# Chunk sums first in the linear attention, spills through other queues, and another opening, in a hybrid attention block

## The chip, the core and the metric

The kernel runs on one core of a Trainium2 chip. The metric is the device time of one execution in microseconds (us); lower is better. TensorE (PE) multiplies matrices, VectorE (DVE), ScalarE (ACT) and GpSimd (POOL) work element by element, and transfers are issued from the queues of SyncE (SP), ACT or POOL. Each engine runs its own instructions strictly in the order in which they stand in its program, and an instruction that has to wait holds back all that stand behind it.

## What is computed

One decoder block on 1024 tokens of width 1024: a softmax attention with low-rank queries and keys (8 heads), beside a gated linear attention (4 heads, keys of 128, values of 256), whose outputs are gated, merged, projected and added to x.

```python
h = rmsnorm(x, g_in)
(c_q, c_kv, k_r, z_mla, q_g, k_g, v_g, a_lr, z_gla, gate_mla, gate_gla) = split(h @ w_in)
# softmax attention: q, k, v from c_q, c_kv (both normalised) and the rotated k_r, causal
y_mla = (softmax_attention(q, k, v) * silu(z_mla)) @ w_proj_mla
# linear attention, head by head, chunk by chunk, b = cumsum of log decay in the chunk
q_in = q_g * exp(b); k_in = k_g * exp(-b); k_st = k_g * exp(b_last - b)
attn = (q_in @ k_in.T) * causal
o = attn @ v_g + q_in @ state                    # within the chunk, and from all before it
state = exp(b_last) * state + k_st.T @ v_g       # from chunk to chunk
y_gla = (rmsnorm(o, g_gla) * silu(z_gla)) @ w_proj_gla
merged = sigmoid(gate_mla) * y_mla + sigmoid(gate_gla) * y_gla
out = rmsnorm(x + merged @ w_out, g_final)
```

Inputs and outputs are float32.

## The kernel before

Every product is taken in three matmuls on a value's rounded part and its remainder (hi·hi, hi·lo, lo·hi); `split` makes the two, the rounded part on ACT (L193) and the remainder on DVE (L194), and for weights `split_raw` (L170, L171, the remainder on DVE or POOL). The 1024 tokens are two halves of 512 (index h). The kernel goes through five stages.

**The opening** (`blocks`, L390 to L505). x is loaded in 16 tiles of 128x512. While they come, PE multiplies zeros 26 times (NWARM, L395). For each half, `squares` squares the eight tiles on ACT and adds them on DVE, `scales` sums over the partitions on PE (L424) and raises the mean to the power -1/2 on POOL (L241), and `spread` copies the row over the partitions on PE (L246). `norm` (L440) scales a tile on DVE and `split` cuts it. The second half's squares stand right behind the first half's tiles in the program.

**The products** (L384). h @ w_in for everything but the gates, by a seven-product scheme on 2x2 blocks whose rows are the token halves; the first two kinds of products (i = 1 and 2) of eight pairs of weight tiles are made early, while the second half of x is still being normalised (`x_steps`), and are spilled to HBM as m1d and c11d. `product` makes twelve matmuls; the results go through `out_q`, `out_k`, `out_v`, `out_silu`, `out_misc` and `out_lat`, which scale, split and transpose them and spill them to HBM (gqd, gvd, szd, crd, latd, krd), through POOL's queue.

**The linear attention** (`core`, L1043 to L1127). Eight groups (two halves of four heads, four chunks of 128 tokens each). `fetch` brings a group's q, k, transposed k and v from HBM by five transfers of 512 KB on POOL's queue, two groups deep. `core` is a generator: scores of the four chunks (tile at), mask and split; then for each chunk its sum k_st.T @ v (tile ups), the outputs of the chunk before (tile ops), and the state (sm, st, split into sh and sl, three slots each); then the norm of the outputs (L241 on POOL, L1113 on ACT); then transposes, the gate, a split (uhl) and a spill of both parts to ugd on POOL's queue. Two groups are advanced in turns, one piece of each per round, and in three rounds of four one step of other work is put in.

That other work is a `Stream` of units, one per weight tile, that yields after every six matmuls. `gate_unit` multiplies x by a tile of the output gates (24 matmuls of 128x512 in four steps); GATES says how many of the 16 gate units of each half stand in front of the units uqr, uv and hi0 to hi3 (which make rotated queries, values, and the queries and keys of a pair of heads), and behind each hi. Fences hold a unit back until its inputs are there.

**The softmax attention** of each half runs over 8 heads: `row_max` of the next head, `scores`, exponentials, `values`, with stream steps between them; before the first head, `row_max(0)` is advanced with one step after each piece. From head 5 on, `linear_inputs` reads ugd back, already split, through POOL's queue. **The end** of each half multiplies by w_proj_gla, w_proj_mla and w_out (units yg, ym, wo).

The kernel's text says what each engine does and in roughly which order; a scheduler then places each engine's instructions by its own timeline of the program. `issue_after` puts instructions behind a given one on their engine.

## Time and profile before

| | |
|---|---|
| time, median of 3 runs | 1120.99 us (1116.2 to 1122.19) |
| the profiled execution | 1117.03 us |
| its span in the trace | 1115.3 us |
| PE, DVE, ACT, POOL busy | 1038.7, 774.5, 583.1, 354.1 us |
| TensorE's clock granted, mean | 0.961 of full speed |

The span goes from the first to the last instruction, and 1.7 us of the profiled execution lie around it. Busy time of PE counts each matmul to its modelled end, so that matmuls overlap; how much work there is shows better in how far apart matmuls start when nothing holds them up. The five stages follow each other on PE: the opening to 36.4 us, the products to 392.7, the linear attention until the first score of the softmax attention at 553.5, the softmax attention and the end of half 0 until about 803, and those of half 1.

### The profile page before, as it was taken

What the parts mean: (1) busy time and instruction counts of PE and PEld (TensorE: products, weight loads), DVE (VectorE), ACT (ScalarE), POOL (GpSimd) and SP (SyncE); (2) the same over time, 40 slices, a digit from 0 to 9 for tenths busy, and PEclk for the clock granted to TensorE, in tenths of its full rate; (3) what the DMA queues carried; (4) which work ended last, traced back from release to release, by engine and by line L of the source; (5) the groups of instructions that cost most, each with busy time, mean ns of one, the idle gap of its engine ahead of it and who ended that gap; (6) DMA issues with size and microseconds to landing.
All of it is one profiled execution on the core that took longest, in us unless ns stands there. A gap on an engine that the chain in (4) does not pass through costs nothing.

```text
span 1115.3 us, 14164 instructions
## 1 busy us (share of the span) xinstructions
PE 1038.7 (93%) x4794; PEld 845.5 (76%) x4794; DVE 774.5 (69%) x1309; ACT 583.1 (52%) x1074; POOL 354.1 (32%) x398
## 2 busy tenths in 40 slices
PE   7999998999999998977699999999899999999995
PEld 4888887878888877766477777888688787777774
DVE  6886667797877666776866766476856768767562
ACT  6644455566565335557666653245556566543332
POOL 0311211111111132532444522323555556432420
PEclk7899999999999999969899999999999999999998
DMA  6652646655645499998733637754933335425331
GB/s 238 217 191 90 228 156 226 232 190 194 216 164 196 170 361 336 339 310 288 256 119 93 212 123 274 255 160 145 201 112 97 105 97 172 153 72 190 122 114 76
DMA packets 80249, 208.74 MB, mean 187 GB/s; under 512 B 8704, under 2 KB 21376, under 8 KB 80048
## 3 DMA queue, kind: packets, MB, share of 16 engines
q1 hardware_dynamic: 47840, 105.18, 29.4%
q0 software_dynamic: 27728, 94.26, 25.2%
q10 hardware_dynamic: 4608, 8.39, 2.0%
q8 instruction: 38, 0.62, 0.2%
q14 instruction: 35, 0.29, 0.1%
HBM read 139.77 MB, written 68.03 MB: 186 GB/s over the span
## 4 chain that ended last, share of the span: by engine, by line
PE 69%; DVE 11%; ACT 7%; issue 6%; DMA 4%; POOL 2%; SPq 0%; POOLq 0%; ACTq 0%; DVEq 0%
PE prod L384 26%; PE pj L184 24%; PE y L895 2%; PE y L894 2%; PE y L893 2%; DMA wraw<-in_dram 2%; DVE pl L1270 2%; PE sc L1257 1%; DVE mx L1220 1%; PE sc L1259 1%; PE sc L1260 1%; PE ov L1279 1%; PE ov L1278 1%; PE sc L1213 1%; DMA xr<-in_dram 1%
## 5 line engine op out<-in xcount | busy, mean ns | idle before, releaser
L184 PE MATMUL pj<-xl,whi 128*128 128x512 f32 x384 | 137.1, 405 | 2.5 <-ACT xl L193 2.1
L170 ACT CAST whi<-wraw 128x1024 fp32r<-128x1024 f32 (+2 forms) x84 | 84.9, 1013 | 84.8 <-PE pj L184 59.9
L1272 POOL TENSOR_TENSOR acc<-acc,p 128x512 f32<-128x512 f32 (+3 forms) x80 | 83.2, 1040 | 111.5 <-ACT p L1266 97.6
L184 PE MATMUL pj<-xh,whi 128*128 128x512 f32 x256 | 104.7, 409 | 3.5 <-ACT whi L170 2.4
L171 POOL TENSOR_TENSOR wlo<-wraw,whi 128x1024 fp32r<-128x1024 f32 (+2 forms) x35 | 78.6, 2247 | 65.3 <-ACT whi L170 35.1
L1270 DVE TENSOR_TENSOR pl<-p,ph 128x512 fp32r<-128x512 f32 (+3 forms) x80 | 73.2, 921 | 31.5 <-ACT ph L1269 31.1
L184 PEld LDWEIGHTS pj<-xl,whi 128*128 128x128 f32 x384 | 75.2, 196 | 18.3 <-ACT xl L193 2.5
L703 DVE TENSOR_TENSOR ring<-prod,ring 128x512 f32<-128x512 f32 x85 | 58.2, 686 | 37.8 <-PE prod L384 37.6
L171 DVE TENSOR_TENSOR wlo<-wraw,whi 128x1024 fp32r<-128x1024 f32 x49 | 63.4, 1297 | 16.4 <-ACT whi L170 16.2
L1266 ACT ACTIVATE p<-sc 128x512 f32<-128x512 f32 (+3 forms) x80 | 37.3, 469 | 68.9 <-DVE sc L1262 46.9
L184 PE MATMUL pj<-lat,whi 128*128 128x512 f32 x264 | 70.2, 400 | 0.7 <-DVE vm L810 0.7
L184 PE MATMUL pj<-xh,wlo 128*128 128x512 f32 x256 | 69.6, 393 | 0.0
L193 ACT CAST w7h<-sw 128x512 fp32r<-128x512 f32 x68 | 42.1, 620 | 50.0 <-PE prod L384 42.1
L1220 DVE TENSOR_REDUCE mx<-sc 128x1 f32<-128x512 f32 (+2 forms) x96 | 52.3, 552 | 21.4 <-PE sc L1213 20.1
L184 PEld LDWEIGHTS pj<-xh,whi 128*128 128x128 f32 x256 | 50.0, 195 | 14.2 <-ACT whi L170 2.8
L384 PE MATMUL prod<-xh,w7h 128*128 128x512 f32 x136 | 56.6, 416 | 2.5 <-ACT ring L715 1.5
L184 PEld LDWEIGHTS pj<-lat,whi 128*128 128x128 f32 x264 | 49.2, 191 | 11.5 <-PE pj L184 1.1
L384 PE MATMUL prod<-xl,w7h 128*128 128x512 f32 x136 | 55.6, 409 | 0.0
L184 PEld LDWEIGHTS pj<-xh,wlo 128*128 128x128 f32 x256 | 47.5, 188 | 9.9
L194 DVE TENSOR_TENSOR w7l<-sw,w7h 128x512 fp32r<-128x512 f32 x68 | 46.4, 683 | 11.0 <-ACT w7h L193 5.7
L193 ACT CAST w7h<-raw 128x512 fp32r<-128x512 f32 x51 | 31.3, 620 | 43.2 <-PE prod L384 33.8
L895 PE MATMUL y<-whi,zl 128*128 128x512 f32 x128 | 50.8, 397 | 0.6 <-DVE zl L194 0.6
(322 smaller groups left out, 2813.1 us busy)
## 6 DMA issues: line engine op xcount, KB each, us to landing
wraw<-in_dram SPq DMA_DIRECT2D x74, 512.0 KB, 3.9
raw<-in_dram SPq DMA_DIRECT2D x32, 512.0 KB, 4.0
gqd<-hl POOLq DMA_DIRECT2D x24, 512.0 KB, 4.6
qk<-gqd POOLq DMA_DIRECT2D x24, 512.0 KB, 8.1
gvd<-hl POOLq DMA_DIRECT2D x16, 512.0 KB, 3.4
vv<-gvd POOLq DMA_DIRECT2D x16, 512.0 KB, 6.4
gtd<-zr ACTq DMA_DIRECT2D x32, 256.0 KB, 2.1
ugd<-uhl POOLq DMA_DIRECT2D x16, 512.0 KB, 5.7
```

Source lines behind the costliest of these rows:

```text
L170: nc.scalar.copy(out=hi[:, 0:n], in_=raw[:, 0:n])
L171: getattr(nc, lo_engine).tensor_tensor(out=lo[:, 0:n], in0=raw[:, 0:n], in1=R(hi[:, 0:n]), op=ALU.subtract)
L184: nc.tensor.matmul(out=ps, lhsT=a, rhs=b, start=(i == 0), stop=(i == 3 * n - 1))
L193: nc.scalar.copy(out=hi, in_=src)
L194: (lo_engine or nc.vector).tensor_tensor(out=lo, in0=src, in1=R(hi), op=ALU.subtract)
L384: nc.tensor.matmul(out=ps, lhsT=a, rhs=b, start=(j == 0 and i in (1, 6, 7, 5)), stop=(j == 11), skip_group_check=True)
L703: nc.vector.tensor_tensor(out=t, in0=ps, in1=y, op=ALU.add)
L895: nc.tensor.matmul(out=c.ops[t], lhsT=a[1], rhs=b[0], start=False, stop=(k == 7))
L1220: nc.vector.reduce_max(mx[:, t, b:b + 1], ps[:, 0:n], axis=mybir.AxisListType.X)
L1266: nc.scalar.activation(p[:, 0:n], ps[:, 0:n], AF.Exp, scale=SCALE)
L1270: nc.vector.tensor_tensor(out=pl[:, 0:n], in0=p[:, 0:n], in1=R(ph[:, 0:n]), op=ALU.subtract)
L1272: nc.gpsimd.tensor_tensor(out=s.acc[:, q0:TH], in0=s.acc[:, q0:TH], in1=p[:, 0:n], op=ALU.add)
```

## The change

It has four parts.

**The opening.** NWARM goes from 26 to 33, nine more multiplications of zeros stand behind the first half's sums and seven behind its spread. The first half's tiles are normalised in turns with their splits: from the third on, a tile's scaling stands behind the remainder of the tile two before. The second half's squares stand behind the first half's last cast, its sums behind the first product, its spread behind the second. One copy is left out in `scales`.

**The queues.** Every transfer that POOL issued is issued by SP (`move`), but for the early products' spills and those of the transposed k, which ACT issues. The reads of m1d and c11d are asked for two products earlier.

**The linear attention.** `core` is replaced by phases of a group that stand in different rounds: scores, all chunk sums and all states in round r; the outputs and the norm in round r+1; the transposes in round r+2. Four stream steps stand in each round. The first state of half 0 is made straight from the sum, without a copy (sm). The group's result is spilled as one float32 tile instead of two parts, and `linear_inputs` splits it when it is read back (eight casts on ACT, eight subtractions on DVE in each half).

**The gates.** In half 0 ten gate units instead of eight stand in front of uqr, and one instead of two behind hi2 and hi3. Four stream steps (one gate unit) stand in front of `row_max(0)` in both halves.

Lines of the diff that only replace `nc.gpsimd.dma_start` by `move` are cut to two of them, and the removed `core` is the one printed above.

```diff
 SLACK = 2
-NWARM = 26
+NWARM = 33
 NS = (1, 1)
-GATES = ((8, 2, 2, 2, 2), (1, 4, 5, 4, 2))
+GATES = ((10, 2, 2, 1, 1), (1, 4, 5, 4, 2))
...
     def split(hi, lo, src, lo_engine=None):
-        nc.scalar.copy(out=hi, in_=src)
-        (lo_engine or nc.vector).tensor_tensor(out=lo, in0=src, in1=R(hi), op=ALU.subtract)
+        cast = nc.scalar.copy(out=hi, in_=src)
+        rest = (lo_engine or nc.vector).tensor_tensor(out=lo, in0=src, in1=R(hi), op=ALU.subtract)
+        return cast, rest
...
+    def move(out, in_, queue=None):
+
+        (queue or nc.sync).dma_start(out=out.bitcast(F32), in_=in_.bitcast(F32))
...
+                zp = mk(mps, [P, TH], F32, "prod")
+
+                def warm_up(mm, n):
+
+                    if first[0] is None:
+                        with tc.issue_after(mm.ins):
+                            for _ in range(n):
+                                nc.tensor.matmul(out=zp, lhsT=zw[:, 0:P], rhs=zw, start=True, stop=True)
...
+                    warm_up(mm, 9)
+                    ms = mk(cst, [P, 4], F32, f"ms{h}")
+                    nc.vector.tensor_scalar(out=ms.unsqueeze(2),
+                                            in0=cps[:, 0:8].rearrange("p (a b) -> p a b", b=2)[:, :, 0:1],
+                                            scalar1=1.0 / D, scalar2=EPS, op0=ALU.mult, op1=ALU.add)
                     rcol = mk(cst, [P, 4], F32, f"rcol{h}")
-                    rsqrt_cols(rcol, ssq, 1.0 / D, cst)
+                    nc.gpsimd.tensor_tensor(out=rcol, in0=ms, in1=mhalf[:, 0:4], op=ALU.pow)
...
+                    warm_up(bcast_row(rcol, None, rb), 7)
...
-                    nc.gpsimd.dma_start(out=(m1d if i == 1 else c11d)[p], in_=t)
+                    nc.scalar.dma_start(out=(m1d if i == 1 else c11d)[p], in_=t)
...
                 rb = spread(scales(0, squares(0)))
+                los = []
                 for kt in range(KT):
-                    norm(0, kt, rb)
-                    split(c.xh[:, kt, :], c.xl[:, kt, :], xr[kt])
+                    if kt < 2:
+                        norm(0, kt, rb)
+                    else:
+                        with tc.issue_after(los[kt - 2].ins):
+                            norm(0, kt, rb)
+                    cast, lo = split(c.xh[:, kt, :], c.xl[:, kt, :], xr[kt])
+                    los.append(lo)
                     if kt in (1, 3):
                         prep(kt // 2)
-                sq1 = squares(1)
                 xs = iter(())
                 for n in range(nearly):
                     if n + 2 < nearly:
                         prep(n + 2)
-                    product(n)
+                    mm = product(n)
                     if n == 0:
-                        rc1 = scales(1, sq1)
+                        first[0] = mm
+                        with tc.issue_after(cast.ins):
+                            sq1 = squares(1)
+                        with tc.issue_after(mm.ins):
+                            rc1 = scales(1, sq1)
                     elif n == 1:
-                        rb1 = spread(rc1)
+                        with tc.issue_after(mm.ins):
+                            rb1 = spread(rc1)
                         xs = x_steps()
...
-                nc.gpsimd.dma_start(out=gqd[h, g, 0], in_=o)
+                move(gqd[h, g, 0], o)
...
-                    nc.gpsimd.dma_start(out=gqd[h, g, 2], in_=u)
+                    move(gqd[h, g, 2], u, nc.scalar)
...
+                if n + 2 < len(seq) and seq[n + 2][0] < NF and begin[seq[n + 2][0]] == n + 2:
+                    s = state[seq[n + 2][0]]
+                    s.m1, s.c11 = ring(), ring()
+                    nc.sync.dma_start(out=s.m1, in_=m1d[seq[n + 2][0]])
+                    nc.sync.dma_start(out=s.c11, in_=c11d[seq[n + 2][0]])
                 if n == begin[p]:
-                    if p < NF:
-                        s = state[p]
-                        s.m1, s.c11 = ring(), ring()
-                        nc.sync.dma_start(out=s.m1, in_=m1d[p])
-                        nc.sync.dma_start(out=s.c11, in_=c11d[p])
...
+        def scores_and_states(h, g):
+            s = Group()
+            s.h, s.g = h, g
+            (s.qh, s.ql, kh, kl, kth, ktl), vv = inputs.pop((h, g))
+            s.v = [(vv[:, :, 0, i, :], vv[:, :, 1, i, :]) for i in range(4)]
             dec = decs[:, g, h, :]
+            aps = mk(gps, [P, 4, P], F32, "at")
             for i, cs in enumerate(css):
+                mm3_now(aps[:, i, :], [((kh[:, cs], kl[:, cs]), (s.qh[:, cs], s.ql[:, cs]))])
+            n = 4 - h
+            ups = []
+            for i in range(n):
+                if i % 2 == 0:
+                    ub = mk(gps, [P, 2, 256], F32, "ups", bufs=2)
+                mm3_now(ub[:, i % 2, :], [((kth[:, css[i]], ktl[:, css[i]]), s.v[i])])
+                ups.append(ub[:, i % 2, :])
+            at = mk(gb, [P, 4, P], F32, "at")
             nc.vector.tensor_tensor(out=at, in0=aps, in1=msk[:, 0:1, :].broadcast_to([P, 4, P]), op=ALU.mult)
+            s.ath = mk(gb, [P, 4, P], F32R, "ath")
+            s.atl = mk(gb, [P, 4, P], F32R, "atl")
+            split(s.ath, s.atl, at)
+            shl = mk(gb, [P, 4, 2, 256], F32R, "shl")
+            s.states = [None] * 4
+            def state(i, src, scalar):
+                st_ = mk(gb2, [P, 256], F32, "st")
+                nc.vector.tensor_scalar(out=st_, in0=src, scalar1=scalar, scalar2=None, op0=ALU.mult)
+                split(shl[:, i, 0, :], shl[:, i, 1, :], st_)
+                s.states[i] = (shl[:, i, 0, :], shl[:, i, 1, :])
+                return st_
+            st_ = state(0, gst[g], dec[:, 0:1]) if h == 1 else None
+            for i in range(n):
+                if st_ is None:
+                    sm = ups[i]
+                else:
+                    sm = mk(gb2, [P, 256], F32, "sm")
+                    nc.vector.tensor_tensor(out=sm, in0=ups[i], in1=st_, op=ALU.add)
+                if i == 3:
+                    nc.vector.tensor_scalar(out=gst[g], in0=sm, scalar1=dec[:, 4:5], scalar2=None, op0=ALU.mult)
+                else:
+                    st_ = state(i + 1, sm, dec[:, i + 1:i + 2])
+            return s
+        def outputs(s):
+            s.oraw = mk(gb2, [P, 4, 256], F32, "oraw")
+            s.oss = mk(gb2, [P, 4], F32, "oss")
+            for o in range(4):
+                if o % 2 == 0:
+                    ops = mk(gps, [P, 2, 256], F32, "ops", bufs=2)
+                prs = [((s.ath[:, o, :], s.atl[:, o, :]), s.v[o])]
+                if s.states[o] is not None:
+                    prs.append(((s.qh[:, css[o]], s.ql[:, css[o]]), s.states[o]))
+                mm3_now(ops[:, o % 2, :], prs)
+                nc.scalar.copy(out=s.oraw[:, o, :], in_=ops[:, o % 2, :])
+                nc.scalar.activation(junk[:, 0:256], s.oraw[:, o, :], AF.Square, accum_out=s.oss[:, o:o + 1])
+        def normalise(s):
+            s.sz = []
+            for f in (2 * s.g, 2 * s.g + 1):
                 t = mk(up, [P, TH], F32, "sz", bufs=2)
+                nc.sync.dma_start(out=t, in_=szd[f, s.h])
+                s.sz.append(t)
             orn = mk(gb2, [P, 4], F32, "orn")
+            rsqrt_cols(orn, s.oss, 1.0 / 256)
             for i in range(4):
+                nc.scalar.activation(s.oraw[:, i, :], s.oraw[:, i, :], AF.Copy, scale=orn[:, i:i + 1])
+        def turn(s):
             for vt in range(2):
+                otp = mk(pj, [P, TH], F32, "pj")
                 for i, cs in enumerate(css):
+                    nc.tensor.transpose(out=otp[:, cs], in_=s.oraw[:, i, vt * P:(vt + 1) * P], identity=idn)
                 uo = mk(gb2, [P, TH], F32, "uo")
+                nc.vector.scalar_tensor_tensor(out=uo, in0=otp, scalar=ggh[:, vt:vt + 1], in1=s.sz[vt],
                                                op0=ALU.mult, op1=ALU.mult)
+                nc.sync.dma_start(out=ugd[s.h, 2 * s.g + vt], in_=uo)
...
+        groups = []
+        for r in range(len(cores) + 2):
+            if 1 <= r <= len(cores):
+                outputs(groups[r - 1])
+            if r < len(cores):
+                groups.append(scores_and_states(*cores[r]))
+            if 1 <= r < len(cores) - 1:
+                fetch(*cores[r + 1])
+            if 1 <= r <= len(cores):
+                normalise(groups[r - 1])
+            if r in (1, 5):
+                sides.append(tables(r // 5))
+            st.step(2)
+            if r >= 2:
+                turn(groups[r - 2])
+            st.step(2)
             for sd in sides:
+                for _ in range(3):
+                    next(sd, None)
...
-                    nc.gpsimd.dma_start(out=slots[f], in_=ugd[h, f])
+                    ur = mk(up, [P, TH], F32, "zr", bufs=2)
+                    nc.sync.dma_start(out=ur, in_=ugd[h, f])
+                    split(slots[f][:, 0, :], slots[f][:, 1, :], ur)
                     c.g.append((slots[f][:, 0, :], slots[f][:, 1, :]))
                     yield
                 st.fences.discard(f"{h}yg0")
 
+            st.step(4)
```

Three places of the engines' programs show what moves. The first is PE's program in the opening; ptr<-one,sw are the sums of the squares (L424, after L441), prod<-idn,rcol the spread of the norms (L246, after L251), prod<-xh and prod<-xl the products (L384, after L390). Before:
```order
L424 MATMUL ptr<-one_72,sw 128x2 x7
L246 MATMUL prod<-idn,rcol_236 128x128 x4
L424 MATMUL ptr<-one_72,sw 128x2 x5
L384 MATMUL prod<-xh,w7h 128x512 x2
L424 MATMUL ptr<-one_72,sw 128x2 x4
L384 MATMUL prod<-xl,w7h 128x512
L384 MATMUL prod<-xh,w7h 128x512
L384 MATMUL prod<-xl,w7h 128x512
L384 MATMUL prod<-xh,w7h 128x512
L424 MATMUL ptr<-one_72,sw 128x2 x4
```

And after the change (the zeros are zw, L408 and L412), with the place of the second half's sums:
```order
L441 MATMUL ptr<-one_72,sw 128x2 x4
L408 LDWEIGHTS zw
L408 MATMUL prod<-zw 128x512
...
L251 MATMUL prod<-idn,rcol_255 128x128 x4
L408 LDWEIGHTS zw
L408 MATMUL prod<-zw 128x512
...
L390 MATMUL prod<-xh,w7l 128x512 x4
L441 MATMUL ptr<-one_72,sw 128x2 x16
L251 MATMUL prod<-idn,rcol_361 128x128 x4
L390 MATMUL prod<-xh,w7h 128x512
```

The second half's sums no longer stand between the first products: they and their spread stand behind 48 products, where 24 stood ahead of the spread before.

The second place is POOL's program in the linear attention; orn is the norm of a group's outputs, wlo a weight's remainder, qk and vv the inputs of coming groups, ugd the result. Before:
```order
L171 TENSOR_TENSOR wlo<-wraw,whi 128x640
L1125 DMA ugd<-uhl 128x1024
L1036 DMA qk_4554<-gqd 128x1024
L171 TENSOR_TENSOR wlo<-wraw,whi 128x1024
L1040 DMA vv<-gvd 128x1024 x2
L1036 DMA qk_4550<-gqd 128x1024
L1036 DMA qk_4662<-gqd 128x1024
L1125 DMA ugd<-uhl 128x1024
L241 TENSOR_TENSOR orn<-ms_4451,mhalf 128x4
L1040 DMA vv<-gvd 128x1024 x2
```

After the change, POOL there (orn is L246 now), and then the queue of SP that holds the transfers (L161 are weights, L203 fetches, L1140 the gates sz, L1156 the results):
```order
L246 TENSOR_TENSOR orn<-ms_4407,mhalf 128x4
L246 TENSOR_TENSOR orn<-ms_4578,mhalf 128x4
L171 TENSOR_TENSOR wlo<-wraw,whi 128x768
L171 TENSOR_TENSOR wlo<-wraw,whi 128x1024
L246 TENSOR_TENSOR orn<-ms_4738,mhalf 128x4
L171 TENSOR_TENSOR wlo<-wraw,whi 128x640
```

```order
L203 DMA qk_4566<-gqd 128x1024
L1140 DMA sz<-szd 128x512 x2
L1156 DMA ugd<-uo 128x512 x2
L161 DMA wraw<-in_dram 128x1024
L203 DMA qk_4568<-gqd 128x1024
L161 DMA wraw<-in_dram 128x1024
L203 DMA vv<-gvd 128x1024
L203 DMA qk_4393<-gqd 128x1024
L203 DMA vv<-gvd 128x1024
```

POOL keeps arithmetic alone, and the results of a group, the fetches of a later one and the weights stand in one queue, one behind the other.

The third place is PE's program in the linear attention; at<-qk are scores, ups a chunk's sum, ops outputs, at<-idn and pj<-idn the transposes, pj<-xh a gate unit. Before:
```order
L1119 MATMUL at<-idn,oraw 128x128 x8
L184 MATMUL ups<-vv,qk_4554 128x256 x3
L1119 MATMUL at<-idn,oraw 128x128 x2
L184 MATMUL ups<-vv,qk_4554 128x256 x3
L1119 MATMUL at<-idn,oraw 128x128 x6
L184 MATMUL ups<-vv,qk_4554 128x256 x3
L184 MATMUL ups<-vv,qk_4662 128x256 x6
L184 MATMUL at<-qk_4550,qk_4552 128x128 x12
```

After the change:
```order
L184 MATMUL pj<-xh,wlo 128x512 x6
L184 MATMUL at<-qk_4393,qk_4395 128x128 x12
L184 MATMUL ups<-vv,qk_4397 128x256 x9
L1152 MATMUL pj<-idn,oraw 128x128 x4
L184 MATMUL ops<-vv,ath 128x256 x2
L184 MATMUL ops<-shl,qk_4393 128x256 x2
```

A group's nine matmuls of sums stand right behind its scores, ahead of any state. Before the change 192 gate matmuls stand up to about the third group's end, and then none but six just ahead of the first score of the softmax attention; after it 240 are spread up to the sixth group, the last two groups have none, and 24 stand ahead of the first of those scores.

## Rows read from the trace of the kernel before

**Rows 1.** The page's first row.
```profile
span 1115.3 us, 14164 instructions
```

**Rows 2.** Windows by stage: length, engines' busy us (instructions), granted clock, DMA share, GB/s.
```profile
core 0: us, PE busy (x) PEld busy (x) DVE busy (x) ACT busy (x) POOL busy (x), PEclk, DMA share, GB/s
0.00:36.40 36.40, 28.96 (x106) 20.69 (x107) 22.48 (x44) 20.25 (x34) 3.01 (x7) 0.72 0.60 211
36.40:392.70 356.30, 351.12 (x1655) 291.04 (x1653) 271.41 (x458) 192.82 (x355) 61.77 (x112) 1.00 0.57 192
392.70:553.50 160.80, 130.37 (x680) 108.52 (x679) 113.94 (x209) 93.12 (x225) 60.79 (x86) 0.89 0.93 314
553.50:674.00 120.50, 113.81 (x533) 92.50 (x534) 79.99 (x180) 73.63 (x129) 47.86 (x48) 0.96 0.44 143
```

**Rows 3.** The chain of work in order of time: start, length.
```profile
36.66 54.89 PE prod L384 x242
```

**Rows 4.** Timeline of the opening: start, length, [idle before, what ended it].
```profile
15.65 2.05 PE L246 MATMUL prod<-idn,rcol 128*128 128x128 f32 x8
...
17.75 5.36 DVE L440 SCALAR_TENSOR_TENSOR xr<-xr,vecs,prod 128x512 f32<-128x512 f32 x8 [2.15 <-PE prod L246]
18.53 0.62 ACT L193 CAST xh<-xr 128x512 fp32r<-128x512 f32 x1 [1.54 <-DVE xr L440]
...
27.84 3.09 DVE L194 TENSOR_TENSOR xl<-xr,xh 128x512 fp32r<-128x512 f32 x5
...
35.61 1.05 PE L246 MATMUL prod<-idn,rcol 128*128 128x128 f32 x8
```

**Rows 5.** PE's groups, 392.7 to 553.5 us: count, busy, mean ns, idle before.
```profile
L184 PE MATMUL pj<-xh,whi 128*128 128x512 f32 x67 | 27.4, 409 | 2.4 <-ACT whi L170 2.4
...
L184 PE MATMUL ups<-vv,qk 128*128 128x256 f32 x84 | 19.9, 352 | 7.4 <-DVE sm L1094 6.3 <-DVE sm L1092 1.0
...
L184 PE MATMUL pj<-xh,wlo 128*128 128x512 f32 x64 | 16.5, 392 | 0.0
...
L184 PE MATMUL ops<-sl,qk 128*128 128x256 f32 x28 | 8.8, 313 | 1.1 <-DVE sl L194 0.9
```

**Rows 6.** PE's timeline at 461 us.
```profile
461.15 1.45 PE L184 MATMUL at<-qk,qk 128*128 128x128 f32 x12
462.44 0.57 PE L184 MATMUL ups<-vv,qk 128*128 128x256 f32 x3
462.84 1.45 PE L184 MATMUL at<-qk,qk 128*128 128x128 f32 x12
```

**Rows 7.** DVE's groups, 392.7 to 553.5 us.
```profile
L194 DVE TENSOR_TENSOR sl<-st,sh 128x256 fp32r<-128x256 f32 x28 | 15.0, 542 | 9.4 <-ACT sh L193 9.3
...
L1094 DVE TENSOR_TENSOR sm<-ups,st 128x256 f32<-128x256 f32 x24 | 10.1, 420 | 12.3 <-PE ups L184 11.9
```

**Rows 8.** POOL's timeline, 505 to 510 us.
```profile
505.78 0.51 POOL L1029 DMA_DIRECT2D krsp<-uhl  x1 [5.23 <-DVE uhl L194]
...
508.89 1.03 POOL L241 TENSOR_TENSOR orn<-ms,mhalf 128x4 f32<-128x4 f32 x1 [0.99 <-DVE ms L240]
```

**Rows 9.** Transfers, 392.7 to 553.5 us: in all; by issue: count, KB, us to landing.
```profile
DMA packets 16431, 50.46 MB, mean 314 GB/s; under 512 B 1921, under 2 KB 2050, under 8 KB 16338
...
qk<-gqd POOLq DMA_DIRECT2D x24, 512.0 KB, 8.1
...
wraw<-in_dram SPq DMA_DIRECT2D x11, 512.0 KB, 7.3
```

**Rows 10.** PE's waits, 553.5 to 803 us: total, times, longest.
```profile
PE sc L1213 <- ACT qt L840: 6.2, 1, 6.2
PE sc L1213 <- DMA ko<-ksp: 2.7, 1, 2.7
```

**Rows 11.** PE's timeline, where the heads begin (L1234) around 650 us.
```profile
646.41 0.40 PE L1234 MATMUL sc<-idr,mt 128*2 128x128 f32 x4 [0.70 <-DVE mt L1229]
...
657.36 0.40 PE L1234 MATMUL sc<-idr,mt 128*2 128x128 f32 x4
```

**Rows 12.** Waits of SP's queue, whole span.
```profile
SPq L329 <- DVE w7l L194: 183.9, 26, 17.6
```

151 lines of the change are left out of this document (31 added, 120 removed).

## The prediction

> **What bounds the kernel now.** The span [rows 1] comes first: 1115.3 us, where the profiled execution took 1117.0, so 1.7 lie around it; the median of the runs is 1121.0, 3.9 above that execution. Next I read the windows by stage [rows 2]. In the products PE is busy for 351.1 of 356.3 us at a granted clock of 1.00, and the chain of waits runs through 242 products on end, 54.89 / 242 = 0.227 us each [rows 3]: that stage is PE's work and little else. In two others PE loses time. In the opening it is busy for 29.0 of 36.4 us at a clock of 0.72, and in the linear attention for 130.4 of 160.8 us at 0.89. Busy time overstates the work, since neighbouring matmuls overlap (0.4 us each, while they start 0.227 apart), so the work of the linear attention must be counted: 255 matmuls of 512 columns (seven groups of the view, the first the 67 of pj<-xh,whi), 264 of 256 columns (five groups, from ups to ops<-sl), 96 of scores, and 64 transposes [rows 5]. They start 0.227, 0.133 (three sums from 462.44 to 462.84) and 0.108 us apart (twelve scores from 461.15 to 462.44) [rows 6]; with 0.11 for a transpose like a score that is 57.9 + 35.1 + 10.4 + 7.0 = 110 us. Some 51 us of the stage are not PE's work. The views that say why come with each part.
>
> **The opening.** In before the second half's spread stands behind 24 products and ends at 36.66 [rows 3, 4]. The first spread takes 2.05 us where the second takes 1.05 [rows 4]: TensorE was at the lower of its two levels (half speed) there, having done no large matmul since the zeros. After the change one copy less stands ahead of it, which I take as 1 us (the power beside it takes 1.03, as orn does in [rows 8]), and nine zero matmuls run in the gap: it starts at 14.6 and takes 1.05 as the second does now, to 15.7 instead of 17.7. On DVE stand then eight scalings of 5.36 / 8 = 0.67 us, eight remainders of 3.09 / 5 = 0.62 and five of weights of about 0.64 [rows 4], 13.5 us, to 29.3; the 48 products end close behind, at 31.5. The second half's squares, eight of about 0.63 behind the last cast on ACT (0.62 each [rows 4]), start at 28.2 and end at 33.2; sums, power and spread follow to about 37.3. So PE leaves the opening 0.7 us later with 24 x 0.227 = 5.4 us more of products done: −4.7. DVE has less room ahead of the second half's tiles, for which I give back 1.7. **−3**, bounds −6 (the slow clock of the opening goes too) and +1 (the products wait for the tiles in their new turns).
>
> **The products.** POOL issued the spills; SP now takes 86 and ACT 24. An issue costs POOL 0.53 us [rows 8]: on SP 46 of 356 us, on ACT 13 beside 192.8 busy [rows 2]. PE has no wait there to lose: **0**, bounds −4 (one stall of the stage goes) and +6 (ACT's results that much later by its queue).
>
> **The linear attention.** Ahead of the first score stand 264 gate matmuls where there were 198, so the work is 110 + 66 x 0.227 = 125 us. What idle time goes? In before each sum waits for the state of the chunk before (sm, 7.3 us of PE's waits [rows 5]), and each link is an addition of 0.42 and a remainder of 0.54 on DVE with a cast between them [rows 7]. POOL's arithmetic stands behind its own transfers: at 505.78 a spill held the queue for 5.23 us for its data, and the norm behind it, a matter of 1.03 us, came at 508.89 [rows 8]. And the last 70 us have no gate matmuls to put under any of it. After the change the sums depend on no state, the outputs come a round later, the norm stands on a queue without transfers, and gate matmuls reach to the sixth group. What stays: 2.4 us for the first weight [rows 5]; for the last two groups, without filler, 7.6: twice a chain of three links of 0.42 + 0.45 and a last split of 0.41 + 0.54, the middle figures taken as close to those of [rows 7], 3.6 us less 0.9 for eight transposes, and once a norm, the power and some 3 us of its neighbours less 2 of a later unit. Then 4 for DVE in the rounds with tables and 7 for transfers that come late, one for each group but the first (both assumed), and 1 small: 22. The 6.2 us that PE waits ahead of the first score [rows 10] are covered by 24 gate matmuls, 5.4. So 125 + 22 = 147, where 160.8 stood: **−14**. Bounds: 135 (the known idle only, 10) and 176 (below).
>
> **The softmax attention of half 0** loses the 66 gate matmuls that moved, 15.0 us. It does not give all back: a head with little filler runs in 11.0 us [rows 11], set by ACT and DVE, and where gates go a head can't shrink below that. I put 4 of the 15 to idle: **−11**, bounds −15 and −7.
>
> **The result read back unsplit.** Sixteen casts and sixteen subtractions come back in the softmax attention, 16 x (0.62 + 0.62) = 19.8 us [rows 4]; the same work leaves the linear attention. DVE has 80.0 of 120.5 us busy there and ACT 73.6 [rows 2], so 40 free, and eight splits in a half want 5 on each. **+2**, bounds 0 and +19.8 (no cover).
>
> **Steps ahead of row_max(0).** The second half's first score waits 2.7 us for a transfer [rows 10]; four stream steps cover it: **−2.7**, bounds −2.7 and 0.
>
> **The sum**: −3 + 0 − 14 − 11 + 2 − 2.7 = −28.7, so 1117.0 − 28.7 = 1088.3 by the profiled execution and 1092.3 by the median. I take **1089**, and 1079 to 1100 for this case alone.
>
> **The rivals.** *Transfers bind the stage.* It moves 50.46 MB at 314 GB/s [rows 9], with a DMA share of 0.93 [rows 2]. Results as one float32 tile spare 16 x 256 KB = 4.2 MB, the added gates bring 2.2: 48.4 MB at today's rate are 154 us, so 7 less gained, 1096. Against it: 314 is a mean over stretches in which nothing was asked for. [...]
>
> *One queue for everything.* A store of results, standing ahead of a later group's fetches and of weights in SP's queue, holds both until its data are there, as the spill did on POOL for 5.23 us [rows 8]. Six fetches held 5 us each, with nothing on PE to put under them, put 30 on 147: 176, and the time at 1118, no change. For it: SP waits up to 17.6 us for one buffer [rows 12]. Against it: groups are fetched a round ahead, 147 / 9 = 16 us.
>
> *The slower side: the spills starve the products of weights.* SP waits 183.9 us in 26 waits for buffers of weights to come free [rows 12], so loads are asked for at once when there is room. 86 spills in that queue wait for their data in turn and hold the loads behind them; if each of some 44 loads comes 1 us late and PE with it, that is +44, to 1133. From 28.7 / 44 = 0.65 us per load on the change loses. Against it: 26 waits of 7 us each are time that the queue has to spare.
>
> *More goes than I count.* The stage comes to 135 us, the heads give back all 15, the opening −6: 1089 − 12 − 4 − 3 = 1070. For it: the idle that I kept (transfers, tables) is assumed, not read. [...]
>
> **How the numbers follow.** Main case 0.54; transfers bind 0.14; one queue 0.12; spills starve the loads 0.10; more goes 0.10. The first, second and last, 0.78, are faster by over 0.5%, about what a measurement of this kernel can tell from no change; one queue is mostly within it; the starved loads are slower, and a hundredth or two of one queue. To leave out 2 in 10 the range goes from 1068, just under the last case, to 1119, the one-queue case, and leaves out the slower side.
>
> **What the changed profile would show.** Right: clock near 1.00 from about 13 us on, first spread of about 1 us; 48 products ahead of the second; first score at about 539 us instead of 553.5; sums (ups) that wait for no sm; orn on POOL within a microsecond or two of its mean; heads in half 0 of about 11 us where gates were taken out. Wrong: PE waiting in the linear attention for qk or vv behind a store on SP; product matmuls waiting for casts of raw weights that landed late; a first score at 550 or later; heads that stay as long as they are with fewer gates in them, or DVE ahead of the second half's tiles at 37 us.

## The result and the profile after

The changed kernel takes 1128.3 us (median of 11 runs) where the kernel before took 1121.0 (11 runs): a ratio of 1.0071, 95% interval 1.0046 to 1.0096. It is slower by 0.7%; 1089 had been forecast, so 39 us of gain did not come.

The table puts the two profiled executions side by side, and two experiments told below, by marks that are the same work in each: the last product, the first score of the softmax attention, the first head of the second half, the first and last matmul of the output projections (y). The column heads 0 goes from the first score to half 0's first y, front 1 from there to half 1's first head, heads 1 from that to half 1's first y.

| kernel | products end | linear attention (gate matmuls ahead of the first score) | heads 0 | front 1 | heads 1 | last y | end |
|---|---|---|---|---|---|---|---|
| before | 392.3 | 161.2 (198) | 165.8 | 88.7 | 240.6 | 53.6 | 13.0 |
| after | 388.1 | 164.3 (264) | 173.8 | 91.8 | 247.3 | 53.9 | 7.2 |
| phases alone (b_lin) | 392.1 | 155.7 (198) | 167.3 | 88.7 | 240.6 | 53.8 | 13.0 |
| after, but for queues and splits (a_pool_pairs) | 388.9 | 161.9 (264) | 166.6 | 92.9 | 236.2 | 53.4 | 13.0 |

Most executions of one kernel lie within 5 us of their median, some up to 10, and the longer ones are mostly those with the lower mean granted clock (of 30 of the kernel before, the shortest, 1117.6 us, had 0.956 and the longest, 1127.7, had 0.950). So a stage of one profile is good to a few us; verdicts rest on the medians, and the stages say where to look. Four of the stages are longer after the change: the linear attention by 3.1 us, heads 0 by 8.0, front 1 by 3.1 and heads 1 by 6.7. The products end 4.3 earlier, and the end is 5.8 shorter, which no term of the prediction had.

The windows by stage of the changed kernel, as [rows 2] (length, busy us and instructions of each engine, granted clock, DMA share, GB/s):

```profile
0.00:36.40 36.40, 32.08 (x145) 19.40 (x145) 23.94 (x44) 21.84 (x38) 1.47 (x6) 1.00 0.66 235
36.40:388.10 351.70, 346.75 (x1636) 287.45 (x1636) 269.82 (x455) 190.65 (x351) 4.80 (x5) 1.00 0.54 189
388.10:552.30 164.20, 137.23 (x747) 115.25 (x746) 99.68 (x192) 92.12 (x216) 20.95 (x14) 0.95 0.84 299
552.30:674.00 121.70, 103.65 (x436) 81.69 (x435) 79.83 (x182) 69.37 (x125) 35.18 (x32) 0.85 0.34 104
```

The opening is at full clock, as forecast, where it was at 0.72. In the last line PE is busy for 104 of 122 us, where it was for 114 of 120, and its clock is 0.85, where it was 0.96: the heads lost their filler and did not get shorter, and TensorE runs more of what is left at its lower level. The timeline of the opening, as [rows 4], has the spread at 1.05 us and the second half's sums behind 48 products:

```profile
14.99 1.05 PE L251 MATMUL prod<-idn,rcol 128*128 128x128 f32 x8
...
32.25 3.63 PE L441 MATMUL ptr<-one,sw 128*128 128x2 f32 x32
...
37.22 1.70 PE L251 MATMUL prod<-idn,rcol 128*128 128x128 f32 x8 [1.35 <-POOL rcol L449]
```

The clock does not stay up, though. PE has to wait for the second spread, and in the stretch behind it the granted clock is 0.80, where it was 1.00 before (first line before, second after); the products start 0.43 us apart from 39.15 us on and 0.23 apart from 43.05:

```profile
36.40:45.00 8.60, 8.60 (x41) 7.12 (x40) 8.46 (x15) 5.26 (x10) 5.39 (x10) 1.00 0.84 306
36.40:45.00 8.60, 7.78 (x31) 6.59 (x32) 6.04 (x10) 3.11 (x6) 0.77 (x1) 0.80 1.00 339
```

PE's groups in the linear attention, as [rows 5]: the sums wait for nothing now, which the phases were for. But the gate units wait 14.7 us for casts of their weights, where it was 2.4.

```profile
L184 PE MATMUL pj<-xh,whi 128*128 128x512 f32 x88 | 38.0, 432 | 15.6 <-ACT whi L170 14.7 <-ACT zr L806 0.9
...
L184 PE MATMUL ups<-vv,qk 128*128 128x256 f32 x84 | 12.0, 286 | 0.0
...
L1152 PE MATMUL pj<-idn,oraw 128*128 128x128 f32 x64 | 11.5, 282 | 5.0 <-ACT oraw L1145 4.6
```

What stands behind that wait shows in two timelines. SP's queue, at the end of the products: six spills of gates take up 16 us, most of it waits for their data, and the weights of the first gate units come behind them, among fetches.

```profile
372.27 16.04 SPq L203 DMA_DIRECT2D szd<-ring  x6
388.40 0.87 SPq L161 DMA_DIRECT2D wraw<-in_dram  x2
389.37 0.38 SPq L991 DMA_DIRECT2D msk<-in_dram  x1
389.84 0.87 SPq L203 DMA_DIRECT2D qk<-gqd  x2
```

ScalarE, a little later: a gate unit's result is ready at 400.9, its transfer is issued at 412.4, and the cast of the next weights stands behind it at 414.4.

```profile
400.31 0.60 ACT L806 ACTIVATE zr<-pj 128x512 f32<-128x512 f32 x1 [5.49 <-PE pj L184]
412.43 0.33 ACTq L807 DMA_DIRECT2D gtd<-zr  x1
412.80 0.60 ACT L806 ACTIVATE zr<-pj 128x512 f32<-128x512 f32 x1 [11.89 <-DMA sz<-szd]
414.07 0.33 ACTq L807 DMA_DIRECT2D gtd<-zr  x1
414.44 1.04 ACT L170 CAST whi<-wraw 128x1024 fp32r<-128x1024 f32 x1 [1.04 <-DMA lat<-latd]
```

In the kernel before the issue stood right behind the result:

```profile
405.90 0.60 ACT L777 ACTIVATE zr<-pj 128x512 f32<-128x512 f32 x1
406.54 0.34 ACTq L778 DMA_DIRECT2D gtd<-zr  x1
406.92 1.05 ACT L170 CAST whi<-wraw 128x1024 fp32r<-128x1024 f32 x1 [0.42 <-ACT zr L777]
```

The semaphores in the trace say why an issue can wait for another transfer. The issues of SP and ScalarE report their landing on eight semaphores, which they take in turn, and an issue stands until the transfer that had its semaphore has landed; the 223 issues of POOL in the kernel before have eight of their own. With POOL's transfers moved, all share eight, and ScalarE's arithmetic stands behind a wait for SP's: the issue at 412.43 takes the semaphore of a fetch of sz that SP issued at 403.25 and that landed at 412.35.

The transfers of the stage ([rows 9]) have not become slower by themselves:

```profile
qk<-gqd SPq DMA_DIRECT2D x24, 512.0 KB, 6.5
...
wraw<-in_dram SPq DMA_DIRECT2D x15, 512.0 KB, 6.5
```

In the softmax attention the wait of 6.2 us ahead of half 0's first score ([rows 10]) is gone and that of 2.7 in half 1 is 1.3; in their place PE waits for DVE and ScalarE inside the heads (the four longest of its waits, 552.3 to 820 us):

```profile
PE sc L1261 <- DVE mt L1256: 4.4, 3, 2.9
PE ov L1305 <- ACT ph L1296: 3.5, 5, 1.9
PE ov L1306 <- DVE pl L1297: 3.1, 4, 1.3
PE sc L1284 <- ACT qt L1264: 2.9, 4, 1.4
```

The head that took 11.0 us in [rows 11] takes 16.3 (first fence), and the chain of waits runs in it through the read-back result and its casts (second):

```profile
648.32 0.40 PE L1261 MATMUL sc<-idr,mt 128*2 128x128 f32 x4
664.64 0.40 PE L1261 MATMUL sc<-idr,mt 128*2 128x128 f32 x4
```

```profile
645.81 3.89 DMA zr<-ugd
649.72 0.63 ACT lat L193
651.09 2.60 DMA zr<-ugd
653.71 0.63 ACT qr L193
```

### The profile page after: what moved, and what is told of

Its sections match the earlier page's. It is cut to its first block, busy times and chain, and to the rows that moved or that the text cites. A ratio compares the mean times of both kernels' runs of the same rounds, so it can differ in the third digit from the quotient of the medians.

```text
span 1126.4 us, 14090 instructions
## 1 busy us (share of the span) xinstructions
PE 1048.0 (93%) x4817; PEld 845.8 (75%) x4817; DVE 762.3 (68%) x1305; ACT 584.6 (52%) x1074; POOL 228.5 (20%) x173
## 4 chain that ended last, share of the span: by engine, by line
PE 37%; DVE 7%; ACT 3%; DMA 3%; issue 2%; POOL 1%; POOLq 0%; DVEq 0%; ACTq 0%; SPq 0%
PE pj L184 23%; PE y L924 2%; PE y L922 2%; PE y L923 2%; PE sc L1284 2%; DVE pl L1297 1%; DVE mx L1247 1%; PE sc L1286 1%; PE sc L1287 1%; PE ov L1306 1%; PE sc L1240 1%; PE ov L1305 1%; DMA zr<-gtd 1%; DMA wraw<-in_dram 1%; DMA kb<-krsp 1%
## 5 line engine op out<-in xcount | busy, mean ns | idle before, releaser
L184 PE MATMUL pj<-xh,whi 128*128 128x512 f32 x256 | 106.1, 414 | 17.1 <-ACT whi L170 14.7
L171 POOL TENSOR_TENSOR wlo<-wraw,whi 128x1024 fp32r<-128x1024 f32 (+2 forms) x33 | 73.6, 2230 | 94.7 <-ACT whi L170 54.3
L1297 DVE TENSOR_TENSOR pl<-p,ph 128x512 fp32r<-128x512 f32 (+3 forms) x80 | 69.7, 878 | 27.1 <-ACT ph L1296 27.0
L171 DVE TENSOR_TENSOR wlo<-wraw,whi 128x1024 fp32r<-128x1024 f32 x51 | 66.3, 1299 | 29.5 <-ACT whi L170 24.4
L246 POOL TENSOR_TENSOR orn<-ms,mhalf 128x4 f32<-128x4 f32 x8 | 8.4, 1049 | 343.5 <-DMA zr<-in_dram 284.1
L184 PE MATMUL pj<-lat,whi 128*128 128x512 f32 x264 | 76.5, 429 | 0.1
L184 PEld LDWEIGHTS pj<-lat,whi 128*128 128x128 f32 x264 | 53.5, 208 | 12.4 <-issue 0.6
L390 PE MATMUL prod<-xl,w7h 128*128 128x512 f32 x136 | 54.1, 399 | 1.4 <-DVE xl L194 1.4
L390 PE MATMUL prod<-xh,w7h 128*128 128x512 f32 x136 | 54.7, 403 | 0.3 <-ACT w7h L193 0.2
```

Of the source, the lines that this page charges most:

```text
L171: getattr(nc, lo_engine).tensor_tensor(out=lo[:, 0:n], in0=raw[:, 0:n], in1=R(hi[:, 0:n]), op=ALU.subtract)
L184: nc.tensor.matmul(out=ps, lhsT=a, rhs=b, start=(i == 0), stop=(i == 3 * n - 1))
L390: mm = nc.tensor.matmul(out=ps, lhsT=a, rhs=b, start=(j == 0 and i in (1, 6, 7, 5)), stop=(j == 11), skip_group_check=True)
L1297: nc.vector.tensor_tensor(out=pl[:, 0:n], in0=p[:, 0:n], in1=R(ph[:, 0:n]), op=ALU.subtract)
```

## The experiments

Three theories were set against each other: **Q**, the queues (weights, fetches and ScalarE wait for each other's transfers); **S**, the splits of the read-back result; **G**, filler taken from heads that do not get shorter for it. Times are medians; the ratio to the kernel before, in brackets with its interval, is from the same chips. A scheduler places the instructions again in every kernel, so each carries some movement besides its edit.

**One part undone in the changed kernel (1128.3).** a_pool: all on POOL's queue again (the first lines of the edit; the other places that named a queue are changed alike).

```diff
-        (queue or nc.sync).dma_start(out=out.bitcast(F32), in_=in_.bitcast(F32))
+        nc.gpsimd.dma_start(out=out, in_=in_)
```

> The changed kernel (1128.3 us) with every moved transfer back on POOL's queue, everything else as changed. Theory Q (one queue: transfers of SP and ScalarE wait for each other, so the gate weights and ScalarE come late at the start of the linear attention): the 14.7 us that PE waits there for casts of weights fall to about 4, the stage from 164 to about 154 us, and the end pays back some 5.5 us because POOL's last drain takes 10 us again, as in the kernel before: about 1123. Theories S (splits of the read-back result set the pace of the heads 5 to 8) and G (gates were taken from heads that ScalarE and VectorE bind): nothing gained in the stage, the end 5.5 us longer, about 1134.

1129.5 [1.0044 to 1.0103]. This is between the two expectations. The waits for casts fall to 2.7 us and the linear attention from 164.3 to 159.6, but the end is 13.0 again: nothing is gained in sum.

a_pairs: the result in two parts again.

```diff
-                nc.sync.dma_start(out=ugd[s.h, 2 * s.g + vt], in_=uo)
+                uhl = mk(gb2, [P, 2, TH], F32R, "uhl")
+                split(uhl[:, 0, :], uhl[:, 1, :], uo)
+                move(ugd[s.h, 2 * s.g + vt], uhl, nc.sync)
...
-                    ur = mk(up, [P, TH], F32, "zr", bufs=2)
-                    nc.sync.dma_start(out=ur, in_=ugd[h, f])
-                    split(slots[f][:, 0, :], slots[f][:, 1, :], ur)
+                    move(slots[f], ugd[h, f], nc.sync)
```

> The changed kernel with the linear attention's result cut into its two parts before it is spilled, as in the kernel before, so that no splits stand in the heads; the queues stay as changed. Theory S: the heads 5 to 8 lose 8 x 1.24 = 10 us of ScalarE and VectorE work in each half, and PE gets most of it back in both halves: about 1112 us. Theory G: in half 0 those heads stay bound without filler, so little comes back there and only half 1 gains: about 1122. Theory Q: 1128, or a little more, since 4 MB more go through the one queue.

1128.5 [1.0036 to 1.0079]. The heads gain most of what S said, 7.0 us in half 0 and 7.5 in half 1, but the linear attention goes from 164.3 to 179.9 (some 6 of this may be that execution's own, 1134.7). SP's queue shows what was missing in all three expectations: a store now waits for its remainder, and fetches and weights behind it.

```profile
SPq L203 <- DVE uhl L194: 12.9, 8, 4.3
```

a_gates: GATES of half 0 as before.

```diff
-GATES = ((10, 2, 2, 1, 1), (1, 4, 5, 4, 2))
+GATES = ((8, 2, 2, 2, 2), (1, 4, 5, 4, 2))
```

> The changed kernel with the gate units of half 0 placed as before (8 ahead, 2 behind each hi), so that 48 gate matmuls, 10.9 us of PE, go back from the linear attention to the heads. Theory G: the heads take them into time in which PE idles now, and the linear attention gets shorter by most of 10.9 us: about 1119. Theory Q: the linear attention waits for transfers and not for PE, so it hardly gets shorter, 1125 to 1128. Theory S: between them, since idle time in the heads is there whatever made it: about 1121.

1128.4 [1.0036 to 1.0091]. With 10.9 us less of PE work the linear attention is as long (164.6). Q forecast that, but waits for transfers are not all of it: PE's idle time there grows by 4.2 us, and its clock falls from 0.95 to 0.90. The heads take 10.9 us more of work in 2.7 us (176.5), at a clock of 0.93 after 0.89.

**Single parts on the kernel before (1121).** b_sp, the queues alone (each `nc.gpsimd.dma_start` to SP or ScalarE as in the change):

> The kernel before (1121.0 us) with only its queues changed: what POOL issued goes to SP, the early products' and the transposed k's spills to ScalarE. Theory Q: the linear attention and the heads come later by some 10 us and the end 5.5 earlier: about 1126. Theories S and G: only the end moves, about 1115.5.

1123.9 [0.9988 to 1.0030], between the two: the linear attention 171.4 (in one of the longest executions, 1129.5), the end 7.1.

b_open, the opening alone:

> The kernel before (1121 us) with the changed opening alone. If the opening is worth what the two traces show (the products end 4.3 us earlier) and nothing behind it eats it: 1117. If the later start of something (weights, decays) eats it: 1121.

1121.3 [0.9977 to 1.0008]. No gain; products end at 391.7 in its profile, only 0.6 us earlier than before.

b_lin, the phases alone (`core` replaced by the printed functions, the result in two parts, all on POOL's queue):

> The kernel before with the linear attention in phases alone: queues, gates, opening and the result's two parts as before. Theory P (the waits for the states were what idled PE): the stage from 161 to about 150 us with the same work, 1110. Theory T (ScalarE, VectorE and the transfers of that stage set its length, and the phases only move the waits): 158 to 165 us, 1118 to 1125.

1113.0 [0.9893 to 0.9941]: nearer to P than to T, with 5.5 us of the stage in the profile. The sums wait for nothing, but PE's idle time in the stage falls only from 30.5 to 28.8 us, and its busy time by 3.9 (the sums take 288 ns each where they took 352). What waits now are outputs and transposes:

```profile
L184 PE MATMUL ops<-vv,ath 128*128 128x256 f32 x64 | 15.2, 330 | 9.7 <-ACT ath L193 8.7 <-ACT oraw L1109 0.9
L184 PE MATMUL ups<-vv,qk 128*128 128x256 f32 x84 | 12.1, 288 | 0.0
L1128 PE MATMUL pj<-idn,oraw 128*128 128x128 f32 x64 | 12.0, 320 | 10.1 <-ACT oraw L1121 8.5 <-ACT zr L782 1.6
```

**The waiting issue and the drain.** a_gtd, the changed kernel:

```diff
-                nc.scalar.dma_start(out=gtd[i], in_=zr)
+                nc.gpsimd.dma_start(out=gtd[i], in_=zr)
```

> The changed kernel (1128.3 us) with one transfer moved: a gate unit's result (gtd), which ScalarE issued and for which its queue stood still for 11.5 us around 412 us, is issued by POOL. Theory A (the issue holds ScalarE, and with it the casts of the next gate weights): PE's 14.7 us of waits for those casts fall below 5, the linear attention from 164 to about 154 us; the end gets 5.8 longer, since POOL issues transfers again: about 1124. Theory B (the weights themselves land late because the transfers run at their highest rate): those waits stay above 10, about 1134.

1128.1 [1.0033 to 1.0073], neither: the waits fall from 14.7 to 9.2 us and the stage stays at 164.0. ScalarE's wait at the issue is real, and taking it away brings nothing in time. In the profile PE's idle time in the stage falls by 4.9 us, and its clock goes from 0.95 to 0.90 and takes them back.

b_tail, the kernel before with POOL's later transfers on SP (`vsp`, `ksp`, `vo`, `ko`, the reads of `krsp` and `ugd`, the second `latd`):

> The kernel before with POOL's transfers behind the linear attention (values, keys, the read-back result, the second half's low-rank inputs) issued by SP, those ahead of it by POOL as before. Theory L (POOL's last drain of 10 us is that of transfers issued late): it falls to about 1 us and the end is 5.8 us shorter: 1115, less what SP's queue costs the heads. Theory N (any transfer on POOL's queue in the program makes it so): the end as before, 1121 to 1124.

1120.1 [0.9965 to 1.0012]: POOL's last drain goes from 10.1 to 6.0 us, which is neither L nor N, and the time stays.

**The other parts on the phases (1113.0).** b_lin_steps (the four steps ahead of `row_max(0)`):

```diff
+            st.step(4)
             marks = st.after
```

> The phases alone (1113 us) with the four stream steps ahead of the first row maxima in both halves, 24 gate matmuls (5.5 us) each. As I predicted: they cover the waits ahead of the first scores (6.2 and 2.7 us) and the heads behind lose them: about 1107. Theory G: what they cover comes back as idle time in the heads: 1113 to 1117.

1114.4 [0.9915 to 0.9969], no gain: G. The phases had already left 1.0 us of the wait of 6.2 ahead of the first score, and that of half 1 stays (2.2 and 2.3 us). In half 1 the first head comes 6.2 us later, and the heads give back 2.4.

b_lin_gates (the changed GATES):

> The phases alone (1113 us) with the changed GATES: 48 gate matmuls, 10.9 us of PE, go from the heads of half 0 into the linear attention. As I predicted: the heads get shorter by most of it and the linear attention takes it into idle time: about 1105. Theory G (the heads stay as long as ScalarE and VectorE need): the heads shorter by some 3 us, the linear attention longer by 0 to 5: 1110 to 1115.

1107.9 [0.9856 to 0.9900], between the two: the linear attention takes 48 gate matmuls at no length (156.0 after 155.7), and heads 0 get shorter by 4.0 of 10.9.

b_lin_one (one tile, read through `zr` and split):

> The phases alone (1113 us) with the result spilled as one tile and split when it is read back, on POOL's queue. Theory S (the splits stand in the heads 5 to 8, which ScalarE and VectorE bind): those heads longer by 7 us in each half, the linear attention a few us shorter for the 16 splits that leave it: about 1122. If the splits are covered there, as I predicted: 1108 to 1113.

1120.1 [0.9967 to 1.0002]: S in sum, by half 1 alone. The linear attention goes from 155.7 to 148.6, heads 0 from 167.3 to 168.4, heads 1 from 240.6 to 251.7; the last three heads of half 1, from start to start, take 24.8, 28.8 and 31.0 us for 21.9, 23.7 and 28.7.

a_pool_pairs (both undone: a_pool and a_pairs together):

> The changed kernel with POOL's queue and the result in two parts again, so with the phases, the opening, the gates and the four steps. The phases alone give 1113. If the queues and the read-back splits ate the rest of it: 1113 to 1116. If the gates and the steps did (theory G, filler taken from heads that do not get shorter for it): 1122 to 1128.

1115.5 [0.9923 to 0.9966]. Queues and splits ate the gain over the phases alone; that the steps cost some more shows further down.

**Which transfers, which half, which opening.** a_pairs with only the products' spills on POOL, and with only fetches, results and later transfers there:

> The changed kernel with the result in two parts (1128.5 us with SP's and ScalarE's queues, 1115.5 with POOL's), and only the spills of the products back on POOL's queue; fetches, results and all later transfers stay on SP's. Theory H (the first gate weights stand behind spills in SP's queue, which wait for their data until the products end): PE's 14 us of waits for casts of gate weights fall below 5, the linear attention by some 9 us, and POOL's last drain gives back 3 to 5: about 1123. Theory F (they stand behind the fetches, of which eight at most are under way): those waits stay above 10: about 1131.

> The same kernel with the other part back on POOL's queue: fetches, results and the later transfers, while the spills of the products stay on SP's and ScalarE's. Theory F: PE's waits for casts of gate weights fall below 5, the linear attention from 180 to about 163, the drain gives back 3 to 5: about 1117. Theory H: they stay above 10, and only what the heads gain comes back: about 1126.

1134.8 [1.0081 to 1.0126] and 1122.2 [0.9984 to 1.0019]: nearer to F. In both the end is long again (12.6 and 12.9 us for 7.2), so that without it the first gains nothing and the second some 12 us. PE's waits for casts of weights in the two:

```profile
PE pj L184 <- ACT whi L170: 10.8, 3, 4.5
```

```profile
PE pj L184 <- ACT whi L170: 7.3, 1, 7.3
```

The stage is 180.1 us with the spills moved back and 169.0 with the fetches; the one wait of 7.3 that stays there, behind the spills, is 4.6 longer than in a_pool_pairs, most of the 7 us to its 161.9, so H has the smaller part.

c_half (half 0's result as one tile, half 1's in two parts) and c_open (opening and early reads):

> The phases with the changed GATES (1107.9 us), and half 0's result alone spilled as one tile and split when it is read back. In the profiles the 16 splits cost the linear attention 7 us, and their read-back cost the heads of half 0 only 1 us and those of half 1 11: if that holds with less filler in half 0, the linear attention gains 3.5 and the heads lose 1: about 1105. If heads with less filler pay for their splits: 1108 to 1112.

1118.6 [0.9951 to 0.9978]: both expectations missed, the first by 14 us. Heads 0 are longer by 3.0 and the linear attention by 1.5 instead of shorter; the rest lies spread over the program, and I can't name its cause.

> The phases with the changed GATES (1107.9 us), the changed opening, and the early products read back two products earlier. If the 4.3 us that the products ended earlier in the changed kernel come from these: about 1104. If they come from the queues, as the kernel with the opening alone says (1121.3): 1108.

1109.2 [0.9857 to 0.9896], no gain: products end 2.0 us earlier and the linear attention takes 3.1 more.

c_more and c_tail:

> The phases with GATES (12, 1, 1, 1, 1) in half 0, so that two gate units more than in the changed table stand ahead of uqr, taken from the heads. The table of the change took 10.9 us of PE into the linear attention at no length (156.0 against 155.7 us) and shortened the heads by 3.9. If there is room for 10.9 more: about 1104. If that room is used up: the linear attention longer by 5 to 8 and the heads shorter by no more than 4: 1109 to 1112.

> The phases with the changed GATES (1107.9 us) and POOL's transfers behind the linear attention issued by SP. The drain of POOL falls from 10.1 to some 6 us, as it did in the kernel before, and with two transfers of a head fewer on a queue that also holds arithmetic the heads stay as they are: about 1104. If SP's queue delays the heads by what the drain gives: 1108 or more.

1109.1 [0.9864 to 0.9911], the linear attention 3.4 us longer and heads 0 unchanged with 10.9 us less of work, at a clock of 0.88 after 0.94: that room is used up. And 1106.5 [0.9858 to 0.9927], with an end of 8.9 for 13.0: not told apart from 1107.9. These, with b_lin_gates and c_open, are the best versions: 1.1 to 1.2% faster than the kernel before, and not told apart from each other.

## Why the prediction was wrong

The runs give a ledger in which each kernel differs from the one above by one part:

| | us | by this part |
|---|---|---|
| kernel before | 1121.0 | |
| phases (b_lin) | 1113.0 | −8 |
| GATES (b_lin_gates) | 1107.9 | −5 |
| opening, early reads (c_open) | 1109.2 | +1 |
| steps ahead of row_max(0) (a_pool_pairs) | 1115.5 | +6 |
| result as one tile (a_pool) | 1129.5 | +14 |
| queues (the change) | 1128.3 | −1 |

By the ratios with their intervals the +1 and the −1 are no difference; the other four are clear of noise. The last two don't add up in any order: from a_pool_pairs the queues cost 13 (a_pairs), and the tile then nothing. By stage the tile costs the heads some 14 us on either queue (2.7 + 11.1, 7.0 + 7.5). The queues cost the linear attention 18.0 with two parts and 4.7 with one tile, where a store waits for no remainder and carries half as much, and they give 5.8 back at the end. That the held stores and the weights behind them make up this difference is argued from SP's waits and the two runs on parts of the queue; no run removes the stores' wait alone.

Filler that moves also moves the clock, for which the prediction had no term outside the opening. The profiles of b_lin and b_lin_gates, which differ by 48 gate matmuls (10.9 us), show it in the linear attention and in heads 0, in this order:

```profile
392.10:547.75 155.65, 126.82 (x681) 108.17 (x679) 104.43 (x204) 94.53 (x226) 58.99 (x84) 0.89 0.92 317
547.75:715.07 167.32, 159.37 (x728) 128.99 (x728) 107.32 (x206) 85.31 (x144) 63.68 (x65) 0.97 0.57 192
```

```profile
391.33:547.30 155.97, 133.00 (x729) 111.72 (x728) 109.78 (x206) 97.11 (x230) 58.71 (x84) 0.96 0.94 327
547.30:710.65 163.35, 152.92 (x679) 122.89 (x680) 104.58 (x206) 81.57 (x140) 59.40 (x63) 0.94 0.55 187
```

Where the matmuls went, the clock rises from 0.89 to 0.96 and PE's idle time falls by 5.8 us; where they came from, the clock falls from 0.97 to 0.94 and idle time grows by 2.5 (7.9 to 10.4). Matmuls of 512 columns start 0.427 us apart at the lower level and 0.229 at the upper (medians over the stream units' matmuls in heads 0 of the changed kernel), so about half of PE's busy time at the lower level is what the clock costs. By that estimate the linear attention gets 7.3 us back (busy at the lower level 27.7, then 13.1) and the heads lose 4.7 (10.2, then 19.6): of the 6.9 us that the heads did not give back, the smaller part is idle time. No run holds the clock fixed, so this split is an estimate and not shown by itself.

The linear attention of a_pool, for the third of the points below:

```profile
390.50:550.14 159.64, 139.58 (x747) 116.23 (x746) 99.94 (x192) 91.43 (x217) 60.09 (x85) 0.95 0.85 296
```

By the steps of the prediction:

- **Opening, −3.** Its parts came as worked out (spread 1.05 us, 48 products ahead of the second), and the 49th product starts 3.4 us earlier than before (38.6 and 42.0), where 4.7 were worked out. But the opening alone brings nothing (0.9993). The step that failed is what is given back behind it, put at 1.7: of the 3.4 us 0.6 are left at the 193rd product (74.0 and 74.6; b_open has 74.2). The runs show the lower clock there (0.80) and a wait of 0.9 us for a remainder of weights; the sum had neither.
- **Products, 0.** The rival of starved weights did not come. From the 193rd product to the last the stage gets 3.6 us shorter (314.1 for 317.7), near the bound of −4, and c_open says that most of it is the early reads: 314.9, where b_open has 317.5. So most of the 4.3 us at the products' end is not the opening's. In time c_open shows none of it. An issue, taken at POOL's 0.53 us, takes about 0.33 on SP and ScalarE.
- **Linear attention, −14.** The stage got 3.1 us longer: 164.3, where 147 was worked out. The sums wait no more, as said. Of the 17 us the queues have 4.7: that is the rival that was given 0.12, one queue for everything, by its mechanism (fetches and weights behind stores, casts behind ScalarE's issue) and far under its price. I had put 7 us on late transfers and found 14.7 in casts of weights alone. The other 12.6 are there on POOL's queue too, in a_pool (the row above). Idle time is 20.1 there, about the 22 put down. The step that failed is the term of the work, 125, where PE is busy for 139.6: some 7 of that is the clock (14.6 us busy at the lower level), and what the other 7 are stays open.
- **Heads of half 0, −11.** The step that failed is the price of the filler: of the 15.0 us taken out only 4 were put to idle time. In a_pool_pairs, without splits, the heads are 0.8 us longer with 15.0 less of work: idle time grows by 6.5 (6.7 to 13.2), and the clock falls from 0.97 to 0.91, by the estimate above some 9.6 (busy at the lower level 9.8, then 29.0), for which the sum had no term. In the change they are 8.0 longer, at 0.89. A head's floor, read from one head of 11.0 us, was no floor of the others; the last three of half 0, from one head's start to the next, now take 18.0, 13.4 and 16.3.
- **The result unsplit, +2.** It costs 7 alone and 14 in the change. The step that failed is the cover: 40 us free on DVE and ScalarE is a mean over the stage, and the splits stand in the heads 5 to 8. That these two engines set the pace there is argued. In heads 1 of b_lin_one the loss, 11.1 us, is near the whole serial length of the splits, 8 x (0.62 + 1.02) = 13.1, while ScalarE waits for the read-back transfers for 1.8 us only; but in heads 0 the same splits cost 1.1, and c_half, 10.7 us slower with heads 0 longer by 3.0, is not explained by it. The upper bound of the prediction, 19.8 for both halves, was the nearer end.
- **Steps ahead of row_max(0), −2.7.** No gain alone, +6 with the rest. The wait at half 1's first score fell in the change (2.7 to 1.3 us) but not in b_lin_steps, and the steps took filler from the heads: from c_open to a_pool_pairs heads 0 get 6.3 us longer, and their clock falls from 0.96 to 0.91.

## What to carry to other kernels

Cover for a moved piece of work has to be read in the window where it will stand, and on a head that is bound by its slower engines nearly the whole serial length can count. Before moving transfers to another queue, list what waits for its data there, and what is issued behind it; here the move cost 13 us where the stores waited for a remainder, more than the 5.8 that it saved at the end. Filler moved between stages is worth what the stage that loses it gives back, measured there, and the granted clock of both stages has to be read beside their idle time.

## What was not expected of the hardware

At the end of the program POOL runs a drain. It took 10.07 us in the kernel before and in the other kernels with POOL's 223 transfers, 0.65 or 0.66 without any, 3.29 with 32, 5.98 with 173, and yet 9.66 with 110 that all stood ahead of 392 us and 9.90 with 113: the end is 7.2 us for 13.0 without POOL's transfers, and what sets the length is open. A remainder of 128x512 on DVE takes 0.68 us, and up to 1.71 when a POOL addition runs at the same time; this pair of rows of b_lin_one (its timeline, heads of half 1) is one of three in eight:

```profile
943.86 1.29 POOL L1275 TENSOR_TENSOR acc<-acc,p 128x512 f32<-128x512 f32 x1 [5.55 <-ACT p L1269]
944.04 1.66 DVE L194 TENSOR_TENSOR lat<-zr,lat 128x512 fp32r<-128x512 f32 x1
```
